# A fused mLSTM, attention and ConvFFN step on one core: a buffer, two loads and three norm steps are moved at the seams of the last two stages

## Chip, cores and metric

The kernel runs on one core of a Trainium2 chip. The metric is the device time of one execution in microseconds (us), as the median of repeated executions. A matmul runs on TensorE (PE; its weight loads are PEld), elementwise work on VectorE (DVE), ScalarE (ACT) and GpSimd (POOL), and SyncE (SP) issues most of the DMAs.

## What is computed

The reference is one layer of an encoder over 2048 prompt tokens and 8 x 16 sample tokens, 17 tiles of 128 tokens in all. Only its last part matters here:

```python
def conv_ffn(h, conv_prev, w_up, w_conv, b_conv, w_down):
    T = h.shape[1]
    u = h @ w_up
    ext = jnp.concatenate([conv_prev.astype(u.dtype), u], axis=1)
    c = b_conv + sum(ext[:, j:j + T] * w_conv[j] for j in range(CONV_W))
    a, g = jnp.split(c, 2, axis=-1)
    return (jax.nn.silu(g) * a) @ w_down, ext[:, -(CONV_W - 1):]
...
    y = layer_norm(DEEPNORM_ALPHA * h + f, ln2_g, ln2_b)
```

The width is 1024, `w_up` has 2 x 2816 columns (value and gate), and the convolution is causal with three taps. All is float32.

## The kernel before

**Products.** Every float32 operand is split into a rounded high part and the rest (`split`: a copy on ACT, L218, and a subtraction on DVE, L219), and a product is the sum high x high + high x low + low x high: three matmuls for one. On top of this the matrix products use a seven-product scheme in place of eight block products (the numbers 1 to 7 named `s` in the code).

**Blocks.** In the ConvFFN the tokens go in three blocks (`FBLOCKS`): tiles 0 to 5, 6 to 11 and 12 to 16. For each block the up-projection (`f_ups`) runs over 22 pairs `j` of a value row and a gate row, 128 columns of `w_up` each. The seven products of a pair (`f_product`, matmul at L1874) collect in three PSUM banks A, B and C of either `fup` (even `j`) or `dps` (odd `j`). `f_evict` takes them out: step 5 copies bank B into `ub` (ACT, L1902) and adds it to bank C to give the second half of the gate row `u1` (DVE, L1903 and L1905); step 4 then adds the rest of bank C, after its product has collected in the same bank, to give the first half (DVE, L1911). The value row goes to `u0`. `f_after` puts the two rows of state ahead of the row (POOL, L1925 and L1927), takes the three taps (ACT, L1929; DVE, L1931 twice), keeps the last rows (POOL, L1932 and L1934), and after the gate row calls `f_gate` (ACT, L1955; DVE, L1956 and L1957), whose result is stored from `cc` to DRAM (L1958, L1960). `u0` and `u1` have one buffer each, so pair `j + 1` can write its gate row only when pair `j` has read its own for the last time. The last pair of the last block has its products in the order 6, 5, 2, 3, 4, with product 4 of the pair before it between 6 and 5.

**Down-projection.** `f_downs` runs over `dseq`: for each block `b` the steps `s` in the order 1, 2, 4, 6, 5, 3, 7 (the last block: 1, 2, 4, 6, 5, 7, 3), and for each step six units `u` of two of the 11 row blocks (the last unit has one). The counter `g` runs over all 3 x 7 x 6 = 126 units. A unit needs split weights (`d_weights`, tile `uw`) and split tokens (`d_tokens`, tile `fu`; for some steps also sums of token quarters, L2038 to L2048). At unit `g` the code asks for the weights of unit `g + 4` and the tokens of unit `g + 5`; the split weights live in a ring of five pairs of buffers. The matmuls are at L2084. After the last unit of a step the result is added to the output rows `yacc` (`add`, L2113 and L2115). Tokens are loaded at L2002, weights at L2020, the rows of the residual at L2139.

**The last norm.** When a tile is complete, `finish` is put on the list `pending`. It is a generator in three pieces: the statistics (L1556 to L1558 on DVE, L1559 on POOL); subtract the mean and multiply by `ln2_g` (L2124); multiply by the scale and add `ln2_b` (L2126), and store (L2127). At each unit `g` the first two of the list go on by one piece. The last step of the last block (`s` = 3, three tiles) uses `norm_last` (L1542, L1544) instead. `ln2_g` and `ln2_b` are loaded at L2060, at the head of `f_downs`, into the two buffers of the tag `hst`, which have held token tiles for the transposes of `f_hT`.

**What sets the order.** PE runs in the order of the code. On every other engine and DMA queue the framework writes a fixed order at build time: it steps through a time of its own and takes, among the instructions that it holds ready, the one traced first; `high_priority` puts `f_evict`'s and `add`'s instructions ahead of others. Each engine then works through its queue in that order, and a waiting instruction holds what is behind it. Buffers of one tag go round in the order of the code.

## Time and profile before

| | |
|---|---|
| median of 3 runs | 2311.37 us |
| the three runs | 2311.37, 2309.41, 2311.43 us |
| the profiled execution, its own time | 2306.19 us |
| its span, first to last instruction | 2304.4 us |
| mean granted clock of PE | 0.997 |
| busy share of the span: DVE / ACT / POOL | 78% / 55% / 12% |

Times in the profile count from the first instruction of the span. A line of a timeline has the start, the time taken, the engine, the line of the program, the operation, the tile written and the tiles read, the shape, and how many were merged; in brackets stands how long the engine sat idle before it and what released it. A line of waits has the waiting engine, tile and line, the releaser, the sum of the idle time, how often, and the longest. A line of the chain of work that ended last has start, time and what.

### The profile page before, as it was taken

The numbers are of one execution on the slowest core, as the hardware profiler recorded it, in microseconds if no ns is written. First come the engines' busy times: TensorE is split into PE (matmuls) and PEld (weight loads), VectorE is DVE, ScalarE is ACT, GpSimd is POOL, SyncE is SP. The second block draws the span as 40 slices with busy tenths as digits, with TensorE's granted clock in tenths as the row PEclk, the third lists the DMA queues.
The fourth block names the chain that finished last, engine by engine and source line by source line (L and its number), as shares of the span: only waits on it lengthen the run. The fifth ranks groups of instructions, "written<-read, shape, count | busy, mean of one in ns | idle before, by whom it ended". The sixth has DMA issues, their size and how long they took to land.

```text
span 2304.4 us, 39746 instructions
## 1 busy us (share of the span) xinstructions
PE 2279.1 (99%) x14293; PEld 2093.5 (91%) x14293; DVE 1807.5 (78%) x3075; ACT 1272.6 (55%) x2377; POOL 272.7 (12%) x509
## 2 busy tenths in 40 slices
PE   8999999999999999999999999999999999999998
PEld 8999999999877778999999999999999988888876
DVE  8787587787688878998778777678766786895987
ACT  4453476776766656555656555555555544444442
POOL 0001001000011210211112100003111200100100
PEclk9999999999999999999999999999999999999999
DMA  7988999999987757888778889978998786756742
GB/s 265 320 303 298 311 321 342 312 305 345 313 285 241 239 196 278 306 320 307 277 276 279 302 307 308 320 263 290 318 293 262 230 294 214 256 167 222 254 154 84
DMA packets 300165, 632.38 MB, mean 274 GB/s; under 512 B 47868, under 2 KB 141120, under 8 KB 299968
## 3 DMA queue, kind: packets, MB, share of 16 engines
q1 hardware_dynamic: 295296, 616.14, 77.8%
q0 software_dynamic: 3520, 10.56, 1.4%
q10 hardware_dynamic: 1152, 3.15, 0.4%
q8 instruction: 113, 1.85, 0.3%
q14 instruction: 84, 0.69, 0.1%
HBM read 458.11 MB, written 171.64 MB: 273 GB/s over the span
## 4 chain that ended last, share of the span: by engine, by line
PE 81%; DVE 4%; DMA 1%; issue 1%; ACT 1%; POOL 0%; SPq 0%; DVEq 0%; ACTq 0%; POOLq 0%
PE dps L1874 19%; PE fup L1874 19%; PE dps L705 7%; PE fup L2084 7%; PE dps L2084 6%; PE fht L2084 6%; PE dps L223 3%; PE dps L224 2%; PE dps L225 2%; PE ppo L1349 1%; PE psc L1304 1%; PE ppt L1343 1%; PE dps L731 1%; PE fht L1698 1%; DVE w L219 1%
## 5 line engine op out<-in xcount | busy, mean ns | idle before, releaser
L1874 PE MATMUL dps<-hh,uw 128*128 128x384 f32 (+1 forms) x1848 | 478.0, 328 | 2.1 <-DVE u L1905 2.1
L1874 PE MATMUL fup<-hh,uw 128*128 128x384 f32 (+1 forms) x1848 | 478.0, 328 | 0.0
L1874 PEld LDWEIGHTS dps<-hh,uw 128*128 128x128 f32 x1848 | 330.0, 188 | 2.4 <-DVE u L1905 2.4
L1874 PEld LDWEIGHTS fup<-hh,uw 128*128 128x128 f32 x1848 | 330.0, 188 | 0.0
L1931 DVE SCALAR_TENSOR_TENSOR cc<-u,cw,cc 128x768 f32<-128x768 f32 (+1 forms) x264 | 257.9, 977 | 63.7 <-ACT cc L1929 56.9
L1874 PE MATMUL fup<-hl,uw 128*128 128x384 f32 (+1 forms) x924 | 302.7, 328 | 0.9 <-DVE hl L219 0.9
L1874 PE MATMUL dps<-hl,uw 128*128 128x384 f32 (+1 forms) x924 | 302.3, 327 | 0.0
L705 PE MATMUL dps<-w,oh 128*128 128x256 f32 x1344 | 254.2, 284 | 0.0
L218 ACT CAST uw<-wraw 128x1024 fp32r<-128x1024 f32 x126 | 123.2, 978 | 231.4 <-PE dps L2084 122.4
L219 DVE TENSOR_TENSOR w<-wraw,w 128x1024 fp32r<-128x1024 f32 (+2 forms) x167 | 189.3, 1140 | 67.0 <-ACT w L218 64.6
L218 ACT CAST w<-wraw 128x1024 fp32r<-128x1024 f32 (+2 forms) x167 | 163.0, 984 | 121.3 <-PE dps L705 63.4
L705 PEld LDWEIGHTS dps<-w,oh 128*128 128x128 f32 x1344 | 210.4, 188 | 10.9 <-issue 8.1
L219 DVE TENSOR_TENSOR uw<-wraw,uw 128x1024 fp32r<-128x1024 f32 x126 | 142.4, 1130 | 65.7 <-ACT uw L218 64.0
L705 PE MATMUL dps<-w,ol 128*128 128x256 f32 x672 | 187.8, 279 | 0.0
L1874 PEld LDWEIGHTS fup<-hl,uw 128*128 128x128 f32 x924 | 173.5, 188 | 1.6 <-DVE hl L219 1.5
L2084 PE MATMUL fup<-uw,fu 128*128 128x512 f32 x726 | 173.7, 396 | 0.0
L1874 PEld LDWEIGHTS dps<-hl,uw 128*128 128x128 f32 x924 | 173.5, 188 | 0.0
L705 PE MATMUL dps<-oh,w 128*128 128x256 f32 x896 | 169.7, 284 | 3.6 <-DVE w L219 1.3
L2084 PE MATMUL dps<-uw,fu 128*128 128x512 f32 x660 | 165.3, 396 | 1.1 <-DVE uw L219 1.1
L2084 PEld LDWEIGHTS fup<-uw,fu 128*128 128x128 f32 x726 | 136.3, 188 | 33.1
L1929 ACT ACTIVATE cc<-u,cw 128x768 f32<-128x768 f32 (+1 forms) x132 | 132.2, 1001 | 49.2 <-DVE u L1911 23.9
L2084 PEld LDWEIGHTS dps<-uw,fu 128*128 128x128 f32 x660 | 123.8, 188 | 31.5 <-DVE uw L219 1.5
(318 smaller groups left out, 4577.9 us busy)
## 6 DMA issues: line engine op xcount, KB each, us to landing
uw<-zw SPq DMA_DIRECT2D x176, 512.0 KB, 5.0
zw<-uw SPq DMA_DIRECT2D x88, 512.0 KB, 3.5
w<-zws SPq DMA_DIRECT2D x72, 512.0 KB, 5.9
wv<-wup SPq DMA_DIRECT2D x66, 512.0 KB, 4.6
wraw<-wi SPq DMA_DIRECT2D x65, 512.0 KB, 6.1
wraw<-zt SPq DMA_DIRECT2D x60, 512.0 KB, 3.9
wraw<-wdn SPq DMA_DIRECT2D x45, 512.0 KB, 4.5
wraw<-wo SPq DMA_DIRECT2D x40, 512.0 KB, 4.7
```

Of the source, the lines that this page charges most:

```text
L218: nc.scalar.copy(hi, src)
L219: nc.vector.tensor_sub(lo, src, hi.bitcast(F32))
L223: mm(out, ah, bh, start=start, stop=False)
L224: mm(out, ah, bl, start=False, stop=False)
L225: mm(out, al, bh, start=False, stop=stop)
L705: mm(o, l, r, start=s in (1, 7) and c == k == i == 0, stop=k == 3 and i == 2, skip_group_check=True)
L731: mm(o, x, w, start=k == i == 0, stop=k == KD - 1 and i == 2, skip_group_check=True)
L1304: nc.tensor.matmul(ps[kvh][:, j, :nk], q[rs, j0 + j], k[rs, sel], start=i == 0, stop=i == 2)
L1874: mm(ps, l[:, k], r[:, k], start=s in (1, 7) and k == 0 and i == 0, stop=k == 3 and i == 2, skip_group_check=True)
L1929: S.activation(c[:, v], u[:, 2:2 + n], AF.Identity, bias=w[3], scale=w[2])
L1931: V.scalar_tensor_tensor(c[:, v], u[:, i:i + n], w[i], c[:, v], op0=ALU.mult, op1=ALU.add)
L2084: mm(ps, l[:, k, c], r[:, k], start=s in (1, 4, 7) and u == 0 and k == 0 and i == 0, stop=u == nu - 1 and k == n - 1 and i == 2, skip_grou ...
```

## The change

Three edits. First, the gate row of the last pair of the last block is put into a buffer of the tag `hst` and not into `u1`. Second, the two loads of the norm's parameters are traced at `g` = 18, the first unit of the fourth step of the first block, and no longer at the head of `f_downs`. Third, in the last block the pieces of `finish` are traced at the end of the unit, after the weights and the tokens that the unit asks for, and within `issue_after(self.low)`: each DVE instruction that the piece traces is put behind the low-part subtraction of the latest weights in the queue. `split` returns that subtraction, and `d_weights` keeps it.

```diff
     def split(self, hi, lo, src):
         nc = self.nc
         nc.scalar.copy(hi, src)
-        nc.vector.tensor_sub(lo, src, hi.bitcast(F32))
+        return nc.vector.tensor_sub(lo, src, hi.bitcast(F32)).ins
...
         elif s == 5:
-            self.ug = u = half(1)
+            end = (b, j) == (len(FBLOCKS) - 1, NFF - 1)
+            self.ug = u = self.fp.tile([P, 770], F32, name="u1", tag="hst", bufs=2) if end else half(1)
...
-        self.split(hi[:, :n], lo[:, :n], raw[:, :n])
+        self.low = self.split(hi[:, :n], lo[:, :n], raw[:, :n])
...
         ln2 = []
-        for n in ("ln2_g", "ln2_b"):
-            t = self.fp.tile([P, D], F32, name="f_" + n, tag="hst", bufs=2)
-            nc.sync.dma_start(t, a[n].to_broadcast([P, D]))
-            ln2.append(t)
...
+        def step():
+            for f in pending[:2]:
+                if next(f, self) is self:
+                    pending.remove(f)
+
         for g, (b, s, u) in enumerate(self.dseq):
...
+            if g == 3 * nu:
+                for n in ("ln2_g", "ln2_b"):
+                    t = self.fp.tile([P, D], F32, name="f_" + n, tag="hst", bufs=2)
+                    nc.sync.dma_start(t, a[n].to_broadcast([P, D]))
+                    ln2.append(t)
...
-            for f in pending[:2]:
-                if next(f, self) is self:
-                    pending.remove(f)
+            if b < nb - 1:
+                step()
             if u == nu - 1 and not last:
                 for p in cols[::-1] if s == 7 else cols:
                     after(s, p)
...
                 self.d_tokens()
+            if b == nb - 1:
+                with self.tc.issue_after(self.low):
+                    step()
```

## The prediction

> **What bounds the kernel now.** I read the page first, then the waits of PE, then the chain of work around the two places that the change touches, and last the timelines of single engines there.

> ```profile
> span 2304.4 us, 39746 instructions
> PE 2279.1 (99%) x14293; PEld 2093.5 (91%) x14293; DVE 1807.5 (78%) x3075; ACT 1272.6 (55%) x2377; POOL 272.7 (12%) x509
> ...
> PE ppt L1518 <- POOL v L1094: 2.9, 1, 2.9
> PE dps L1874 <- DVE u L1905: 2.1, 1, 2.1
> ...
> PE dps L2084 <- DVE uw L219: 1.1, 1, 1.1
> ...
> PE fht L2084 <- DVE yacc L2115: 0.2, 1, 0.2
> ```

> PE is busy for 2279.1 of 2304.4 us, and the edits leave its matmuls alone. So the change can only win PE's idle time, 25.3 us over the whole span, and of that only what lies in the last two stages. There PE waits three times: 2.1 us for the gate row (L1905), 1.1 us for a weight split (L219), 0.2 us for an addition. The 2.9 us of L1518 belong to an earlier stage. After PE's last matmul come a last norm and its store. The third edit doesn't reach them, because `norm_last` is called inside the product loop as before. The most that the change can win is thus 2.1 + 1.1 + 0.2 = 3.4 us, 0.15% of the span.

> **Part 1, the gate row in its own buffer.** The first wait, from the chain, then from the timelines of ACT, PE and DVE:

> ```profile
> 1823.18 3.53 PE dps L1874 x24
> ...
> 1829.96 0.35 DVE u L1903
> 1830.31 0.21 DVE u L1905
> ...
> 1830.56 2.02 PE dps L1874 x12
> ```
> ```profile
> 1825.24 0.41 ACT L1902 COPY ub<-dps 128x320 f32<-128x320 f32 x1
> ```
> ```profile
> 1828.14 0.30 PE L1874 MATMUL dps<-hh,uw 128*128 128x320 f32 x1
> 1830.56 0.42 PE L1874 MATMUL dps<-hh,uw 128*128 128x320 f32 x1 [2.12 <-DVE u L1905]
> ```
> ```profile
> 1825.04 1.21 DVE L219 TENSOR_TENSOR uw<-wraw,uw 128x1024 fp32r<-128x1024 f32 x1
> 1826.18 0.89 DVE L1931 SCALAR_TENSOR_TENSOR cc<-u,cw,cc 128x656 f32<-128x656 f32 x1
> 1827.14 1.23 DVE L219 TENSOR_TENSOR uw<-wraw,uw 128x1024 fp32r<-128x1024 f32 x1
> 1828.28 0.90 DVE L1931 SCALAR_TENSOR_TENSOR cc<-u,cw,cc 128x656 f32<-128x656 f32 x1
> 1829.09 0.95 DVE L219 TENSOR_TENSOR fu<-r,fu 128x768 fp32r<-128x768 f32 x1
> 1829.96 0.35 DVE L1903 TENSOR_TENSOR u<-dps,ub 128x192 f32<-128x192 f32 x1
> ```

> The last pair's step 4 collects in the bank that L1903 and L1905 read, so PE waits for L1905. Their data is there at 1825.24 + 0.41 = 1825.65. They run 4.3 us later because `u1` still holds the row before, whose second tap (L1931) ends at 1828.28 + 0.90 = 1829.2. With a buffer of its own only `ub` is left to wait for. L1903 is high in priority, so it goes behind the split of 1825.04, which ends at 1826.25, and the two (0.35 + 0.21) are over by about 1826.9. PE wants the bank when its last matmul before the gap ends, 1828.14 + 0.30 = 1828.4: a cover of 1.5 us, and the 2.12 us go. Should one split more (1.23) get ahead of them, the cover still holds; should a tap get ahead as well (0.9), some 0.6 us of wait would stay. Bounds of this term: 0 to 2.12 us; I take 2.12. No instruction is added.

> What is late next? The first units of the down-projection have their splits done by then; the nearest is the first token unit of the second step:

> ```profile
> 1848.13 1.83 DVE L219 TENSOR_TENSOR fu<-r,fu 128x768 fp32r<-128x768 f32 x2
> ```
> ```profile
> 1833.06 46.20 PE fup L2084 x198
> ...
> 1883.46 2.80 PE dps L2084 x12
> ```
> ```profile
> 1831.00:2156.00 325.00, 325.00 (x1398) 261.63 (x1398) 260.06 (x314) 142.84 (x175) 18.72 (x19) 1.00 0.68 230
> ```
> ```profile
> 1876.47 1.22 DVE L219 TENSOR_TENSOR uw<-wraw,uw 128x1024 fp32r<-128x1024 f32 x1
> ```

> The 46.20 us are two steps of 99 matmuls, so the second begins at 1833.06 + 23.1 = 1856.2, and its tokens are split by 1850.0: 6.2 us of cover. The tightest that I find is the weight split of unit 13, over at 1877.7 for a product at 1883.46: 5.8 us, or 3.7 once PE comes 2.1 us earlier. Behind the seam PE is busy for 325.00 of 325 us (the row of a table by stretches: PE, PEld, DVE, ACT, POOL, clock, DMA share, GB/s), so the 2.12 us arrive at the end whole.

> **Part 2, the parameters loaded later.** Before, the loads went out long ahead:

> ```profile
> 1475.91 0.38 SPq L2060 DMA_DIRECT2D f_ln_g<-ln_g  x1
> ...
> 1492.10 0.38 SPq L2060 DMA_DIRECT2D f_ln_b<-ln_b  x1
> ```
> ```profile
> f_ln_g<-ln_g SPq DMA_DIRECT2D x1, 512.0 KB, 8.0
> ```
> ```profile
> L2124 DVE SCALAR_TENSOR_TENSOR yacc<-yacc,lmv,f_ln_g x14: 1271/1274/1279, 1977.1 to 2281.7; 128x1024 f32<-128x1024 f32 x14
> ```
> ```profile
> 1836.54 0.90 DVE L1931 SCALAR_TENSOR_TENSOR cc<-u,cw,cc 128x656 f32<-128x656 f32 x1
> ```
> ```profile
> 1843.88 4.24 SPq L2002 DMA_DIRECT2D r<-zf  x8
> ```
> ```profile
> 1860.00:1870.00 10.00, 10.00 (x45) 8.05 (x44) 8.99 (x11) 3.98 (x5) 0.00 (x0) 1.00 1.05 405
> ```

> One `hst` buffer now holds the gate row until its last tap ends at 1836.54 + 0.90 = 1837.4, so at least one load falls behind that. First use is L2124 at 1977.1, far off. On SP each issue takes 0.38 us, and the row loads behind it wait until 1843.88 anyway. A load is 0.5 MB; at 405 GB/s the two take 2.6 us of DMA time, in a stretch where the DMA engines are full. That is under the 3.7 us of cover left at unit 13: cost 0. From the other side, if everything behind were late by each load's 8.0 us to land, 16 us, it would break the cover (a rival below). Taking the loads away from 1476 to 1492 wins nothing, since PE has no wait there. I take 0, as the bandwidth row is that of the stretch itself. [...]

> **Part 3, the norm steps behind the splits.** Around the second wait, DVE, ACT and PE:

> ```profile
> 2274.27 1.22 DVE L219 TENSOR_TENSOR uw<-wraw,uw 128x1024 fp32r<-128x1024 f32 x1
> 2275.41 0.95 DVE L219 TENSOR_TENSOR fu<-r,fu 128x768 fp32r<-128x768 f32 x1
> 2276.28 1.87 DVE L1556 BATCH_NORM_STATS2 lst<-yacc 128x6 f32<-128x512 f32 x3
> ...
> 2278.78 1.22 DVE L219 TENSOR_TENSOR uw<-wraw,uw 128x1024 fp32r<-128x1024 f32 x1
> ...
> 2280.52 2.47 DVE L2124 SCALAR_TENSOR_TENSOR yacc<-yacc,lmv,f_ln_g 128x1024 f32<-128x1024 f32 x2
> 2282.91 0.68 DVE L219 TENSOR_TENSOR uw<-wraw,uw 128x512 fp32r<-128x512 f32 x1
> ```
> ```profile
> 2276.77 0.62 ACT L218 CAST uw<-wraw 128x512 fp32r<-128x512 f32 x1 [2.45 <-PE fht L2084]
> ```
> ```profile
> 2283.64 0.73 PE L2084 MATMUL dps<-uw,fu 128*128 128x512 f32 x2 [1.08 <-DVE uw L219]
> ```

> The three `uw` rows are the weights of units 123, 124 and 125. The last has its high part at 2277.4 and could be split then, but stands behind both L2124; PE pays 1.08 us. Does the edit turn this round? I follow the code. Before, the tiles come on the list at the end of unit 119; the pieces run in units 120, 121, 122, each ahead of the weights that its unit asks for (124, 125, none). After, they run at the end of units 119, 120, 121, behind weights 123, 124, 125. Both give: weights 123, statistics, weights 124, L2124, weights 125, L2126. The edges ask only for what the order has already: L2124 behind weights 124, not 125. So the wait stays, and this part gives 0 here; its bounds are 0 and 1.08.

> It does move something at the start of the last block, where three tiles of the block before are still on the list: their pieces go from ahead of the weights of units 88 to 93 to behind them. DVE's work is the same in sum. A split needs its buffers freed by PE, so the pieces wait a few us more; but behind them stand splits wanted four units (16.8 us) later, and no matmul waits for the norm: 0.

> **Sum.** 2306.19 - 2.12 = 2304.1 us for an execution like the profiled one (span 2302.3). The median shown, 2311.37, is 5.2 us above that execution, so the same step on it gives 2309.25, said as 2309.3 us: 0.09% less.

> **The rivals.**
> - *Both waits go*: the framework's order, made from its own times, puts weights 125 ahead of L2124. For it: the high part is there 3.1 us before L2124 starts. Against: the code traces L2124 first. 2311.37 - 2.12 - 1.08 = 2308.2 us.
> - *The change doesn't do what it says*: something else holds L1903, such as a second tap and splits queued ahead of it, so that PE waits as long. For it: between 1825 and 1830 DVE has hardly a gap. Against: the priority of `f_evict`. 2311.4 us.
> - *Slower: the late loads starve the weights.* If each load holds back what is behind it by its 8.0 us, unit 13 is late by 16 - 3.7 = 12.3 us; less 2.1 gained, the time is 2311.4 + 10.2 = 2321.6 us. It decides from the point where the delay passes 3.7 us, and the kernel is slower than before past 5.8 us. For it: the DMA engines are full there. Against: 2.6 us of traffic.

> **Chances and range.** Forecast 0.70, both waits 0.12, no gain 0.12, slower 0.06. The three runs lie 2.0 us apart, and the profiled execution lies 5.2 below their median, so a median can be off by 2 to 3 us. Low: 2308.2 less half of 5.2, 2305.6. High: no gain plus half of 2.0, 2312.4; the slow rival is left out. A measurement of this kernel tells about 0.2% (4.6 us) from no change. Faster by more needs a median under 2306.7, beyond even both waits: 0.11, by the scatter. Slower by more: 0.06. Within: 0.83.

> **What would show it.** Part 1: PE's wait for L1905 gone, L1903 near 1826, the down-projection starting near 1831. Part 2: one load at least behind 1835, no wait of PE at L2084 between 1831 and 2200. Part 3: the wait for L219 still about 1.1 us, with L2124 ahead of the 512-wide split. I am wrong if a new wait shows behind 1831, or if the splits at the end stand in another order.

## The result and the profile after

| | before | after |
|---|---|---|
| median | 2308.07 us (22 runs, 2303.73 to 2311.43) | 2305.24 us (22 runs, 2302.08 to 2310.27) |
| profiled execution, its own time | 2306.19 us | 2306.25 us |
| its span | 2304.4 us | 2304.5 us |

The ratio is 0.9987, with a 95% interval of 0.9981 to 0.9992: the change takes off 2.8 us (1.8 to 4.4). The interval leaves out a change of nothing, and the difference is inside the 0.2% (4.6 us) that the prediction gave as most likely. The predicted 2309.3 us lies 4.1 us above the median measured, and the low end of the range 0.4 us above it.

The lines of the program have moved a little: L1903, L1905 and L1931 are now L1904, L1906 and L1932; the matmul L2084 is L2081, the copies L2092 are L2089, L2124 is L2121, and the loads of the norm's parameters stand at L2145.

The two profiled executions have the same span, so the change is to be read stage by stage. First the waits of PE in the kernel after, around the seam and to its end:

```profile
PE fup L2081 <- ACT fht L2089: 1.2, 1, 1.2
...
PE dps L2081 <- DVE uw L219: 1.1, 1, 1.1
```

The 2.1 us at L1905 are gone, and the 1.1 us for the weight split are still there. New is a wait of 1.2 us at the second step of the down-projection, where PE needs a bank that ACT's copies (L2089) have not yet emptied.

**The seam.** DVE in the kernel after, and then two moments of PE in each kernel (the product 4 of the pair before the last, and the first matmul of the down-projection), before first:

```profile
1826.01 1.22 DVE L219 TENSOR_TENSOR uw<-wraw,uw 128x1024 fp32r<-128x1024 f32 x1
1827.14 0.35 DVE L1904 TENSOR_TENSOR u<-dps,ub 128x192 f32<-128x192 f32 x1
1827.41 0.28 DVE L1906 TENSOR_TENSOR u<-dps,ub 128x128 f32<-128x128 f32 x1
1827.61 0.89 DVE L1932 SCALAR_TENSOR_TENSOR cc<-u,cw,cc 128x656 f32<-128x656 f32 x1
```
```profile
1821.25 0.31 PE L1874 MATMUL fup<-hh,uw 128*128 128x320 f32 x1
...
1832.89 1.33 PE L2084 MATMUL fup<-uw,fu 128*128 128x512 f32 x5
```
```profile
1822.21 0.32 PE L1874 MATMUL fup<-hh,uw 128*128 128x320 f32 x1
...
1831.48 1.79 PE L2081 MATMUL fup<-uw,fu 128*128 128x512 f32 x7
```

The gate row's additions now stand ahead of the second tap, one split later than forecast, and PE does not wait for them. From product 4 to the first matmul of the down-projection it was 1832.89 - 1821.25 = 11.64 us and is 1831.48 - 1822.21 = 9.27 us: 2.37 us less. I call this stretch the seam. The wait read 2.12 us in the trace; the seam lost more, because the last matmul ahead of the gap is recorded as 0.30 us long and the first behind it as 0.42 us, while such matmuls otherwise start 0.17 us apart or less (12 of them in 2.02 us, by the chain before).

**Behind it.** From the first matmul of the down-projection to the end of the span it was 2304.4 - 1832.89 = 471.5 us and is 2304.5 - 1831.48 = 473.0 us: 1.5 us more. That is where the gain went. ACT in the kernel after, then PE:

```profile
1849.15 0.84 ACT L218 CAST fu<-r 128x768 fp32r<-128x768 f32 x1 [3.84 <-DMA r<-zf]
...
1852.09 0.84 ACT L218 CAST fu<-r 128x768 fp32r<-128x768 f32 x1 [0.42 <-DMA r<-zf]
1853.61 0.83 ACT L218 CAST fu<-r 128x768 fp32r<-128x768 f32 x1 [0.69 <-DMA r<-zf]
1854.35 1.04 ACT L218 CAST uw<-wraw 128x1024 fp32r<-128x1024 f32 x1
1855.30 1.06 ACT L2089 COPY fht<-fup 128x512 f32<-128x512 f32 x2
```
```profile
1855.93 6.34 PE L2081 MATMUL fup<-uw,fu 128*128 128x512 f32 x26 [1.21 <-ACT fht L2089]
```

The copies start 1855.30 - 1831.48 = 23.8 us behind the first matmul of the step, whose 99 matmuls take 23.1 us. Ahead of them in ACT's queue stand token casts that wait for row loads (`r<-zf`). In the kernel before, with the first matmul at 1832.89, the copies came at 22.2 us:

```profile
1854.09 1.05 ACT L218 CAST uw<-wraw 128x1024 fp32r<-128x1024 f32 x1 [1.44 <-PE fup L2084]
1855.05 1.06 ACT L2092 COPY fht<-fup 128x512 f32<-128x512 f32 x2
```

There the cast ahead of them waited for PE itself, not for a load. The first of the two copies was over at about 1855.6, half of 1.06 us behind 1855.05, and PE wanted its bank at 1832.89 + 23.1 = 1856.0: a cover of 0.4 us, which the prediction had not looked for.

Why do the rows come later? SP's queue in the kernel after, and the time that the last store of the convolution's rows took to land, after and before:

```profile
1837.68 0.33 SPq L2145 DMA_DIRECT2D f_ln_b<-ln_b  x1
1838.72 0.38 SPq L2021 DMA_DIRECT2D wraw<-zt  x1
1840.34 0.33 SPq L1959 DMA_DIRECT2D zf<-cc  x1
1840.72 0.43 SPq L1961 DMA_DIRECT2D zf<-cc  x1
1842.17 0.37 SPq L2021 DMA_DIRECT2D wraw<-zt  x1
1845.79 3.94 SPq L2003 DMA_DIRECT2D r<-zf  x8
```
```profile
zf<-cc SPq DMA_DIRECT2D x1, 64.0 KB, 5.0
```
```profile
zf<-cc SPq DMA_DIRECT2D x1, 64.0 KB, 3.1
```

What the row loads waited for in SP's queue, from 1835 to 1850 us, after and before:

```profile
SPq L2003 <- DMA zf<-cc: 3.1, 2, 2.4
```
```profile
SPq L2002 <- DMA zf<-cc: 2.5, 2, 1.8
```

The row loads read what the store of 1840.72 writes, so they start when it has landed. It lands in 5.0 us where it took 3.1, and 3.0 us ahead of it the 512 KB of `ln2_b` (tile `f_ln_b`) are issued. By the packets in the trace these run from 1838.87 to 1842.63 us, and those of the store begin 2.5 us behind its issue, where they began 1.5 us behind it before. The trace has the packets of both on one queue (q1). Whether the store shares the DMA engines with the load or stands behind it in that queue, no run here tells; that it is this load is shown below (one_behind). Together with the seam (the store now starts 9.2 us behind the first matmul, before 1840.72 - 1832.89 = 7.8) the row loads begin 14.3 us behind the first matmul, before 11.0.

**The end.** DVE in the kernel after, and PE:

```profile
2280.55 2.47 DVE L2121 SCALAR_TENSOR_TENSOR yacc<-yacc,lmv,f_ln_g 128x1024 f32<-128x1024 f32 x2
2282.94 0.68 DVE L219 TENSOR_TENSOR uw<-wraw,uw 128x512 fp32r<-128x512 f32 x1
```
```profile
2283.67 0.73 PE L2081 MATMUL dps<-uw,fu 128*128 128x512 f32 x2 [1.08 <-DVE uw L219]
```

The same order and the same 1.08 us as before: the third part does nothing here.

### The profile page after: what moved, and what is told of

Same layout as the page of the kernel before. It is cut to its first block, busy times and chain, and to the rows that moved or that the text cites. A ratio compares the mean times of both kernels' runs of the same rounds, so it can differ in the third digit from the quotient of the medians.

```text
span 2304.5 us, 39741 instructions
## 1 busy us (share of the span) xinstructions
PE 2278.9 (99%) x14293; PEld 2094.4 (91%) x14293; DVE 1807.4 (78%) x3075; ACT 1272.4 (55%) x2377; POOL 279.4 (12%) x509
## 4 chain that ended last, share of the span: by engine, by line
PE 81%; DVE 4%; DMA 2%; issue 1%; ACT 1%; POOL 0%; SPq 0%; DVEq 0%; ACTq 0%; POOLq 0%
PE dps L1874 19%; PE fup L1874 19%; PE dps L705 8%; PE fup L2081 6%; PE dps L2081 6%; PE fht L2081 6%; PE dps L223 3%; PE dps L224 2%; PE dps L225 2%; PE ppo L1349 1%; PE psc L1304 1%; PE ppt L1343 1%; PE dps L731 1%; PE fht L1698 1%; PE pscore L1129 1%
## 5 line engine op out<-in xcount | busy, mean ns | idle before, releaser
L1874 PE MATMUL fup<-hh,uw 128*128 128x384 f32 (+1 forms) x1848 | 478.4, 328 | 0.0
L1874 PE MATMUL dps<-hh,uw 128*128 128x384 f32 (+1 forms) x1848 | 478.0, 328 | 0.0
L1874 PEld LDWEIGHTS fup<-hh,uw 128*128 128x128 f32 x1848 | 330.5, 188 | 0.0
L1874 PEld LDWEIGHTS dps<-hh,uw 128*128 128x128 f32 x1848 | 330.3, 188 | 0.0
L1932 DVE SCALAR_TENSOR_TENSOR cc<-u,cw,cc 128x768 f32<-128x768 f32 (+1 forms) x264 | 258.2, 979 | 62.8 <-ACT cc L1930 56.1
L1874 PE MATMUL fup<-hl,uw 128*128 128x384 f32 (+1 forms) x924 | 303.2, 328 | 0.9 <-DVE hl L219 0.9
L1874 PE MATMUL dps<-hl,uw 128*128 128x384 f32 (+1 forms) x924 | 302.8, 328 | 0.0
L705 PE MATMUL dps<-w,oh 128*128 128x256 f32 x1344 | 254.2, 284 | 0.0
L218 ACT CAST uw<-wraw 128x1024 fp32r<-128x1024 f32 x126 | 123.3, 979 | 230.4 <-PE dps L2081 122.4
L219 DVE TENSOR_TENSOR w<-wraw,w 128x1024 fp32r<-128x1024 f32 (+2 forms) x167 | 189.7, 1142 | 66.0 <-ACT w L218 61.9
L218 ACT CAST w<-wraw 128x1024 fp32r<-128x1024 f32 (+2 forms) x167 | 163.0, 984 | 119.0 <-PE dps L705 61.9
L705 PEld LDWEIGHTS dps<-w,oh 128*128 128x128 f32 x1344 | 210.7, 188 | 10.8 <-issue 8.1
L219 DVE TENSOR_TENSOR uw<-wraw,uw 128x1024 fp32r<-128x1024 f32 x126 | 142.5, 1131 | 62.3 <-ACT uw L218 62.2
L705 PE MATMUL dps<-w,ol 128*128 128x256 f32 x672 | 188.1, 280 | 0.0
L1874 PEld LDWEIGHTS fup<-hl,uw 128*128 128x128 f32 x924 | 173.9, 188 | 1.7 <-DVE hl L219 1.5
L2081 PE MATMUL fup<-uw,fu 128*128 128x512 f32 x726 | 174.0, 396 | 1.2 <-ACT fht L2089 1.2
L1874 PEld LDWEIGHTS dps<-hl,uw 128*128 128x128 f32 x924 | 173.8, 188 | 0.0
L705 PE MATMUL dps<-oh,w 128*128 128x256 f32 x896 | 169.6, 285 | 3.6 <-DVE w L219 1.3
L2081 PEld LDWEIGHTS fup<-uw,fu 128*128 128x128 f32 x726 | 136.6, 188 | 34.3 <-ACT fht L2089 1.6
L2081 PE MATMUL dps<-uw,fu 128*128 128x512 f32 x660 | 165.3, 396 | 1.1 <-DVE uw L219 1.1
L1930 ACT ACTIVATE cc<-u,cw 128x768 f32<-128x768 f32 (+1 forms) x132 | 132.0, 1001 | 46.2 <-DVE u L1912 22.2
L2081 PEld LDWEIGHTS dps<-uw,fu 128*128 128x128 f32 x660 | 124.1, 188 | 31.2 <-DVE uw L219 1.5
## 6 DMA issues: line engine op xcount, KB each, us to landing
uw<-zw SPq DMA_DIRECT2D x176, 512.0 KB, 5.1
zw<-uw SPq DMA_DIRECT2D x88, 512.0 KB, 3.3
w<-zws SPq DMA_DIRECT2D x72, 512.0 KB, 5.8
wv<-wup SPq DMA_DIRECT2D x66, 512.0 KB, 4.4
wraw<-wi SPq DMA_DIRECT2D x65, 512.0 KB, 5.5
wraw<-zt SPq DMA_DIRECT2D x60, 512.0 KB, 4.1
wraw<-wdn SPq DMA_DIRECT2D x45, 512.0 KB, 4.5
wraw<-wo SPq DMA_DIRECT2D x40, 512.0 KB, 4.7
```

Source lines behind the costliest of these rows:

```text
L218: nc.scalar.copy(hi, src)
L219: return nc.vector.tensor_sub(lo, src, hi.bitcast(F32)).ins
L705: mm(o, l, r, start=s in (1, 7) and c == k == i == 0, stop=k == 3 and i == 2, skip_group_check=True)
L1874: mm(ps, l[:, k], r[:, k], start=s in (1, 7) and k == 0 and i == 0, stop=k == 3 and i == 2, skip_group_check=True)
L1930: S.activation(c[:, v], u[:, 2:2 + n], AF.Identity, bias=w[3], scale=w[2])
L1932: V.scalar_tensor_tensor(c[:, v], u[:, i:i + n], w[i], c[:, v], op0=ALU.mult, op1=ALU.add)
```

## The experiments

All of these kernels compute the full result. "Seam" and "to the end" are the two stretches above, from the profile of each kernel. The difference in time is the ratio less 1, times the median of before that was run beside the kernel.

| kernel | median (runs), before beside it | ratio (95%) | difference, us | seam | to the end |
|---|---|---|---|---|---|
| row_dead | 2305.77 (11), 2308.44 | 0.9989 (0.9980 to 0.9998) | -2.5 | 9.26 | 471.5 |
| loads_behind | 2306.29 (11), 2308.44 | 0.9995 (0.9987 to 1.0004) | -1.2 | 9.26 | 471.5 |
| no_row | 2309.34 (11), 2308.44 | 1.0003 (0.9994 to 1.0012) | +0.7 | 12.35 | 472.3 |
| norm_behind | 2307.27 (11), 2308.44 | 0.9999 (0.9990 to 1.0007) | -0.2 | 13.12 | 470.7 |
| after_again | 2307.70 (11), 2308.89 | 0.9993 (0.9985 to 1.0002) | -1.6 | 9.26 | 473.1 |
| fill_gap | 2308.36 (11), 2308.89 | 0.9999 (0.9991 to 1.0008) | -0.2 | 11.65 | 471.5 |
| wide_gap | 2314.91 (10), 2308.89 | 1.0021 (1.0011 to 1.0030) | +4.8 | 18.85 | 471.8 |
| dead_behind | 2305.91 (11), 2308.89 | 0.9985 (0.9975 to 0.9995) | -3.5 | 9.26 | 470.7 |
| one_behind | 2306.02 (10), 2309.51 | 0.9983 (0.9974 to 0.9993) | -3.9 | 9.26 | 471.5 |
| row_hst | 2306.32 (10), 2309.51 | 0.9988 (0.9978 to 0.9997) | -2.8 | 9.26 | 475.9 |
| steps_only | 2308.08 (10), 2309.51 | 0.9999 (0.9989 to 1.0009) | -0.2 | 11.65 | 471.5 |
| before_again | 2308.36 (10), 2309.51 | 0.9996 (0.9986 to 1.0005) | -0.9 | 11.64 | 471.5 |
| row_hst_again | 2307.33 (10), 2308.18 | 0.9997 (0.9987 to 1.0006) | -0.7 | 9.26 | 472.4 |
| after_third | 2306.05 (10), 2308.18 | 0.9992 (0.9983 to 1.0002) | -1.8 | 9.26 | 472.3 |
| before_third | 2308.14 (10), 2308.18 | 1.0002 (0.9993 to 1.0012) | +0.5 | 12.35 | 472.4 |

The runs beside these experiments are not those of the table of the result. The intervals are about 4 us wide, so times alone separate few of these kernels; the two copies of the kernel before show -0.9 and +0.5 us. The stretches of the profile decide, and the times are held against their sum.

### The gate row without the late loads

The kernel before, with the gate row in the buffer `hh5`, which holds no live tile by then, so that the norm's parameters load early as before:

```diff
-            self.ug = u = half(1)
+            end = (b, j) == (len(FBLOCKS) - 1, NFF - 1)
+            self.ug = u = f2.tile([P, 770], F32, name="u1", tag="hh5", bufs=1) if end else half(1)
```

> The kernel before with one edit: the last pair's gate row goes into the buffer of the tokens of product 5, which are dead by then. The parameters keep their early loads and the norm steps their place. The gate row's wait (2.4 us start to start) goes by both theories. Theory A (the parameters' late loads delay the token rows, and ACT's copies behind them make PE wait 1.2 us at the second step): no wait of PE for the copies of L2089; 2.4 us faster, ratio about 0.9990. Theory B (the delay comes from the weights load that now stands ahead of the token rows on SP, which this kernel has too): the wait for the copies stays at 0.5 to 1.2 us; 1.0 to 1.9 us faster, ratio about 0.9994.

Measured: seam 9.26 us, to the end 471.5 us as in before, no wait for the copies, 2.5 us faster. With this buffer the first part wins its whole gap; the loss behind the seam does not come from an earlier start of the down-projection alone.

### The loads behind the row loads

The kernel after, with both norm loads queued behind the row loads of the first step:

```diff
-        self.nc.sync.dma_start(r[:, ks, :h], z[:, :, c0:c0 + h])
+        self.rows = self.nc.sync.dma_start(r[:, ks, :h], z[:, :, c0:c0 + h]).ins
...
-                    nc.sync.dma_start(t, a[n].to_broadcast([P, D]))
+                    with self.tc.issue_after(self.rows):
+                        nc.sync.dma_start(t, a[n].to_broadcast([P, D]))
```

> The changed kernel with its two parameter loads put behind the token row loads of the first block on SP's queue; the weights load ahead of the rows stays. Theory A: the first row load goes out near 1844 instead of 1845.8, no wait of PE for the copies, 1.2 to 1.4 us faster than the changed kernel's profile, ratio to before about 0.9990. Theory B: rows still late by over 1 us and a wait of 0.5 to 1.2 us at the copies.

The waits of PE from the seam to the end of this kernel, and the landing of the last store:

```profile
PE dps L2081 <- DVE uw L219: 1.1, 1, 1.1
PE fht L2081 <- DVE yacc L2112: 0.2, 1, 0.2
```
```profile
zf<-cc SPq DMA_DIRECT2D x1, 64.0 KB, 3.3
```

No wait for the copies, the store lands in 3.3 us, and the row loads start 12.6 us behind the first matmul, in the changed kernel 14.3. The weight load that stands ahead of the row loads is still there, so it is not what costs. The time, 1.2 us less than before, is not as good as the forecast; that is left open below.

### Only the second load behind

The same edit for `ln2_b` alone:

```diff
-                    nc.sync.dma_start(t, a[n].to_broadcast([P, D]))
+                    with self.tc.issue_after(self.rows) if n == "ln2_b" else nullcontext():
+                        nc.sync.dma_start(t, a[n].to_broadcast([P, D]))
```

> The changed kernel with one load alone, ln2_b, queued behind the row loads of the down-projection's first step; ln2_g stays among the weight loads ahead of it. Theory (the copies of the first step's result, L2089 on ACT, wait because the token casts ahead of them wait for row loads that the ln2_b load has pushed back): the first row load is issued at most 13.3 us behind the first down-projection matmul (14.3 in the changed kernel, 13 or less where both loads lie behind), and PE's wait for the copy in the first 30 us of the down-projection, 1.2 us in the changed kernel twice, is under 0.4 us. Rival (the load of ln2_g, or any load among the weights, costs as much): the row load is still about 14.3 us behind, and the wait 0.6 to 1.2 us. Time by the theory 1.2 us under the changed kernel's, ratio to before about 0.999; by the rival as the changed kernel.

Measured: the row loads start 12.5 us behind the first matmul, there is no wait for the copies, to the end 471.5 us, 3.9 us faster. `ln2_g`, which goes out at the start of the seam, is harmless; the new wait is the work of `ln2_b`, issued just ahead of the last stores. This is the changed kernel without its new wait; by their times alone the two cannot be told apart.

### Without the first part, and the third part alone

no_row is the kernel after with the gate row back in `u1`:

```diff
-            end = (b, j) == (len(FBLOCKS) - 1, NFF - 1)
-            self.ug = u = self.fp.tile([P, 770], F32, name="u1", tag="hst", bufs=2) if end else half(1)
+            self.ug = u = half(1)
```

> The changed kernel without its first edit: the gate row is back in u1, the loads are traced late, the norm steps stand behind the splits. If the first edit is all that acts, PE waits 2.1 us for the gate row as before, the parameters load near 1476 and 1492 as before, and the time is that of the kernel before, ratio 0.9995 to 1.0005. Rival: the second and third edits win something of their own (the measured gain of 2.8 us is more than the 2.1 forecast): 0.5 to 1 us faster, ratio about 0.9997.

steps_only is the kernel before with the pieces of the norm traced as after:

```diff
-            for f in pending[:2]:
-                if next(f, self) is self:
-                    pending.remove(f)
+            if b < nb - 1:
+                step()
...
+            if b == nb - 1:
+                with self.tc.issue_after(self.low):
+                    step()
```

> Part 3 alone: the norm's steps of the last block queued behind the splits, the gate row in u1 and the loads early. All theories: the wait for the gate row 2.1 us and the wait for the weight split before the last steps 1.1 us stay, no wait for the copies; ratio to before 0.9995 to 1.0010. Open: whether the gap also halves the clock of PE behind it (two of three kernels with the gap so far): if so the seam takes 12.3 to 13.2 us or the first matmuls of the down-projection are slow, and if not it takes 11.64.

Measured: both have the gap of 2.12 us and the 1.1 us at the end, and neither is faster than before. With the gate row in `u1` the two `hst` buffers are free, and the loads go out early wherever they are traced. So the second part costs nothing by its place in the code; it is the first part's buffer that makes the second load late. no_row showed a surprise: its seam took 12.35 us, not 11.64, with the clock at 0.50 behind the gap. That is taken up below.

### The first edit alone, in the buffer of the changed kernel

The gate row in the `hst` buffer, and all else as before: the loads are traced at the head of `f_downs`, and still go out late, because one of their two buffers holds the gate row:

```diff
-            self.ug = u = half(1)
+            end = (b, j) == (len(FBLOCKS) - 1, NFF - 1)
+            self.ug = u = self.fp.tile([P, 770], F32, name="u1", tag="hst", bufs=2) if end else half(1)
```

> Parts 1 and 2 without part 3: the gate row in the hst buffer, the two loads traced at the head of the down-projection, the norm's steps as before. Theory (the buffer that the row takes pushes the loads back, whatever the place where they are traced): the seam takes 9.26 us as in the changed kernel, and the wait for the copies (1.2 us) is there in full. Rival (the place where the loads are traced, or part 3, brings the wait of the copies): that wait is under 0.4 us. Ratio to before 0.9987 to 0.9995 by the theory.

> Parts 1 and 2 again (the gate row in the hst buffer, no part 3). Open: its first profile had a wait of 2.55 us for the copies, behind which the clock fell to 0.50 for 3.41 us, while its median was 0.12% under the kernel before. Theory (the wait comes from row loads that land late, so its length differs from execution to execution, from about 1.2 us up): here it lies between 0.5 and 2.6 us, with DMA as releaser of the token casts ahead of the copies. Rival (without part 3 the wait is always 2.5 us): 2.5 us again. Clock, by the theory of windows: PE's clock is looked at in a fixed grid of 3.413 us windows, the grid being that of the profile's other low stretches; the window behind one with under about 1.45 us of busy PE runs at 0.50, behind one with over 1.63 us at 1.00.

The wait of PE for the copies, in row_hst and then in its second profile:

```profile
PE fup L2085 <- ACT fht L2093: 2.5, 1, 2.5
```
```profile
PE fup L2085 <- ACT fht L2093: 0.6, 1, 0.6
```

The wait is there without the second and the third edit, and its length differs from execution to execution of one program. The rival, a fixed 2.5 us without part three, falls.

### The changed kernel again

> The changed kernel once more, for a second profile. By the measure from the start of the pair before the last's product 4 to the first matmul of the down-projection, called the seam: 9.3 us and clock 1.00 there, as in its first profile. If the wait at the copies (1.35 us start to start) belongs to the kernel and not to one execution, it is there again, 1.0 to 1.5 us, and from the first matmul of the down-projection to the end it takes 473 us; if it was an accident, 471.5 us. Time against before: ratio 0.998 to 0.9995.

> The changed kernel, unchanged, a third profile. Theory: the wait for the copies is there again, 0.5 to 2.6 us; below 1.7 us of it the clock stays at 1.00. Rival (it is a fixed 1.2 us): 1.2 us again. Ratio to before 0.998 to 0.9995.

Measured: a wait for the copies of 1.2 us in the second profile and of 0.5 us in the third, whose row is:

```profile
PE fup L2081 <- ACT fht L2089: 0.5, 1, 0.5
```

It belongs to the kernel and is not fixed. In all five profiles that have the second load ahead of the stores (three of the changed kernel, two of row_hst) the store took 4.7 to 5.4 us to land (5.0, 5.4 and 4.9, then 5.3 and 4.7); in five without it 3.1 to 3.3 (before 3.1, before_third 3.2, row_dead 3.2, dead_behind 3.1, loads_behind 3.3). In before_again, no_row and fill_gap, which lack it too, the row loads that wait for the store begin 3.1 to 3.3 us behind its issue.

### The norm's steps really behind the last weights

The third part meant to spare PE the last split. This kernel is before with the pieces of the last step queued behind the last weight split:

```diff
-            for f in pending[:2]:
-                if next(f, self) is self:
-                    pending.remove(f)
+            if not last:
+                step()
...
+            if last:
+                with self.tc.issue_after(self.low):
+                    step()
```

> The kernel before with the norm pieces of the last step only traced at the end of their unit and queued behind the latest weight split, so that L2124 stands behind the weights of the last unit. If the 1.1 us wait before the last products is the price of that order, it goes, PE ends 1.1 to 1.2 us earlier and the kernel is 1.1 to 1.2 us faster, ratio about 0.9995. Rival: VectorE is the bound in the last 25 us, its work is only reordered and the end stays: ratio 1.000, with PE idle elsewhere or the last norm late by as much.

The last additions on DVE in this kernel:

```profile
2297.03 0.74 DVE L1544 SCALAR_TENSOR_TENSOR yacc<-yacc,lsc,f_ln_b 128x512 f32<-128x512 f32 x1
2298.37 0.69 DVE L2113 SCALAR_TENSOR_TENSOR yacc<-yacc,fht 128x512 f32<-128x512 f32 x1 [0.60 <-PE fht L2084]
2298.98 0.74 DVE L1544 SCALAR_TENSOR_TENSOR yacc<-yacc,lsc,f_ln_b 128x512 f32<-128x512 f32 x1
```

The wait of 1.1 us is gone and the way to the end is 470.7 us, 0.8 less. The rest is given back: a last piece of the tile before (2298.98) now stands between the last addition and the last tile's statistics, and from the last addition to the end it takes 7.9 us, before 7.4. The time itself (-0.2 us, -2.3 to +1.6) does not tell this kernel from before.

### Both waits removed

row_dead and norm_behind together.

> The two edits that worked alone together: the gate row in the dead token buffer, the norm pieces of the last step behind the last weight split. Seam 9.3 us, no wait at the copies, no wait before the last products; from the first matmul of the down-projection to the end 470.7 us (471.5 less the 0.8 that the order of the norm won). Against before 2.4 to 3.9 us at the seam and 0.8 at the end: 3.2 to 4.7 us faster, ratio about 0.9983; if seam and end don't add, 0.9990.

Measured: seam 9.26, to the end 470.7, both as short as in any kernel here; 3.5 us faster (1.2 to 5.8). Its time cannot be told from one_behind's.

### The gap filled, and the gap widened

fill_gap puts 15 matmuls into the gap, whose result nothing reads; wide_gap writes the second half of the gate row seven times. Both start from the kernel before.

```diff
+            if (b, j, s) == (nb - 1, NFF - 1, 4):
+                hole = self.fup.tile([P, 512], F32, name="fht", tag="fht", bufs=2)
+                for _ in range(15):
+                    nc.tensor.matmul(hole[:, :320], self.wc[b, j, s][0][:, 0], self.hc[b, s][0][:, 0], start=True, stop=True, skip_group_check=True)
```
```diff
-            V.tensor_add(u[:, 2 + h:2 + WP], C[:, :m], u4[:, :m])
+            for _ in range(7 if (b, j) == (len(FBLOCKS) - 1, NFF - 1) else 1):
+                V.tensor_add(u[:, 2 + h:2 + WP], C[:, :m], u4[:, :m])
```

> The kernel before with 15 more matmuls of PE (results unused, in a free PSUM bank) in the place where it waits for the gate row, 2.2 us in all, so that PE is busy in the gap. Theory G (in part of the executions the gap also halves PE's granted clock for some 3 us, which costs 0.8 to 1.5 us more): the seam takes 11.6 to 11.9 us and the clock is 1.00 from 1830 to 1840. Theory S (the longer seams are scatter of VectorE's work and not of the clock's gate): the seam is as in the kernel before, 11.6 to 13.1 us, and a lower clock may show. The time is that of before or up to 1 us less.

> The kernel before with the second half of the last pair's gate row written seven times instead of once (the same values), which makes VectorE 1.6 us later there, so that PE's gap at the seam is about 4 us instead of 2.4. Theory G: the clock is 0.5 behind the gap for about 3.4 us, and the seam takes 11.6 + 1.6 + 1.5 = 14.5 to 15 us. Theory S: clock 1.00, the seam takes 13.2 us, or up to 14.7 with the same scatter. 1.6 to 3 us slower than before, ratio 1.0007 to 1.0013.

Measured: filled, the seam keeps its 11.65 us and the clock stays at 1.00. Widened, PE waits 7.4 us, not 4, because DVE's queue puts splits, taps and the gate's steps between the seven additions. The clock is at 0.50 for 10.2 us, and the kernel is 4.8 us slower (2.5 to 6.9). The seam is 7.2 us longer than in a profile of before at full clock; the runs of before that stand beside it may include some whose clock falls as well, as it does in before_third below.

### The kernel before again

> The kernel before, unchanged, for another profile of it. Ratio 1.000 within 0.001. If the gap of 2.1 to 2.4 us halves PE's clock in some executions of a kernel and not by the kernel's code, this profile may show either 11.64 us for the seam at a clock of 1.00 throughout, as the first profile of it did, or 12.3 to 13.2 us with slices of 0.50 to 0.72 within 6 us behind the gap. If it is the code, it must be 11.64 again.

> The kernel before, unchanged, a third profile. All theories: the wait for the gate row is 2.12 us. Theory of windows: the clock falls to 0.50 for 3.41 us if and only if one window of the fixed grid holds about 1.9 us or more of the gap, and the seam with the first product then takes 1.4 to 1.7 us more; else the seam is 11.64 us. Rival (chance, with no bearing on the grid): the two don't go together.

before_again has a seam of 11.64 us at full clock, before_third one of 12.35 us with the clock at 0.50 behind the gap: the same program shows both. With no_row, norm_behind and steps_only there are six profiles with this gap, three of either kind.

What tells them apart? In before the trace has a clock of 0.50 in three stretches: from 10.58 us for 6.83 us, from 41.30 us for 3.41 us, and from 2300.93 us to the end. Their starts lie 30.72 and 2259.62 us apart, which is 9 and 662 steps of 3.4133 us; the changed kernel has the same two distances, from 10.18 to 40.90 and on to 2300.52 us. So I lay a grid of windows of this length over each profile, with one edge at the start of one of its low stretches. Here it is over the gap by a table of stretches (PE, PEld, DVE, ACT, POOL, clock, DMA share, GB/s), in before, steps_only, no_row and before_third:

```profile
1826.47:1829.89 3.42, 1.98 (x14) 1.72 (x12) 3.35 (x4) 1.97 (x6) 1.61 (x3) 1.00 0.61 166
1829.89:1833.30 3.41, 2.74 (x16) 2.60 (x17) 3.32 (x8) 1.58 (x4) 1.81 (x5) 1.00 0.62 231
```
```profile
1828.34:1831.76 3.42, 1.64 (x12) 1.38 (x10) 3.35 (x5) 2.17 (x5) 1.62 (x5) 1.00 0.60 192
1831.76:1835.17 3.41, 3.07 (x18) 2.84 (x19) 3.32 (x7) 1.59 (x3) 1.47 (x3) 1.00 0.62 235
```
```profile
1830.34:1833.76 3.42, 1.44 (x10) 1.44 (x11) 3.42 (x7) 2.81 (x5) 2.77 (x6) 1.00 0.57 195
1833.76:1837.17 3.41, 3.41 (x11) 2.83 (x11) 2.96 (x5) 0.93 (x1) 0.00 (x0) 0.50 0.41 153
1837.17:1840.58 3.41, 3.41 (x16) 2.77 (x15) 2.39 (x3) 0.00 (x0) 0.00 (x0) 1.00 0.48 118
```
```profile
1830.57:1833.98 3.41, 1.45 (x10) 1.45 (x11) 3.41 (x7) 2.79 (x5) 2.76 (x6) 1.00 0.60 199
1833.98:1837.40 3.42, 3.42 (x11) 2.84 (x11) 2.98 (x5) 0.93 (x1) 0.00 (x0) 0.50 0.42 155
```

In before and steps_only the gap is shared out between two windows, PE is busy for 1.98 and 1.64 us of the emptier one, and the clock stays at 1.00. In no_row and before_third one window holds nearly all of the gap, PE is busy for 1.44 and 1.45 us of it, and the window behind runs at 0.50: 11 matmuls in it, where the next one of no_row at 1.00 has 16. norm_behind goes with these two (1.41 us busy, then 0.50), and so does row_hst, whose wait of 2.5 us lay within one window (0.88 us busy, then 0.50). In the changed kernel the wait of 1.2 us left PE busy for 2.21 us of its window, and the clock stayed at 1.00. The last two, row_hst first:

```profile
1852.39:1855.81 3.42, 0.88 (x4) 0.38 (x2) 2.40 (x3) 3.14 (x5) 0.00 (x0) 1.00 1.05 398
1855.81:1859.22 3.41, 3.40 (x8) 2.75 (x9) 2.41 (x3) 3.07 (x5) 0.00 (x0) 0.50 1.05 407
```
```profile
1853.37:1856.78 3.41, 2.21 (x10) 1.47 (x9) 2.73 (x3) 3.17 (x5) 0.00 (x0) 1.00 1.04 393
1856.78:1860.20 3.42, 3.42 (x16) 2.77 (x15) 2.55 (x3) 2.21 (x5) 0.00 (x0) 1.00 1.05 405
```

before_third was profiled after these two bounds had been put down as an expectation, and agrees with them. In fill_gap the 15 matmuls run from 1834.65 to 1837.00 us, wholly within one window of its grid:

```profile
1833.86:1837.27 3.41, 3.41 (x24) 3.22 (x23) 3.41 (x7) 2.42 (x5) 1.89 (x5) 1.00 0.82 279
1837.27:1840.69 3.42, 3.42 (x21) 3.05 (x20) 3.42 (x6) 1.02 (x2) 0.88 (x2) 1.00 0.47 170
```

Without them nearly the whole gap would have lain in that window, as in no_row; with them the clock behind it stays at 1.00. One profile, but it speaks for the reading that the fall goes with PE's idle time in the window. The two bounds, 1.45 and 1.64 us, are however those of this place. Near the start of before, where PE runs other matmuls (L705), 1.90 us of busy PE were not enough:

```profile
37.89:41.30 3.41, 1.90 (x14) 1.49 (x13) 3.41 (x6) 2.95 (x4) 0.00 (x0) 1.00 0.98 393
41.30:44.71 3.41, 3.41 (x18) 3.41 (x18) 3.41 (x6) 0.94 (x1) 0.00 (x0) 0.50 0.70 223
```

Busy time as the profile models it thus does not tell all cases apart, and what else counts was not shown. What the window at 0.50 cost is read from no_row and before_third: 0.7 us more in the seam and 0.8 us more to the end, 1.5 us. In norm_behind it falls into the seam as a whole (13.12 against 11.64).

## Why the prediction was right or wrong

**Part 1** was right in its mechanism and too small in its size. The wait went, the additions moved ahead of the tap, the cover held with one split more ahead of them, and the down-projection began at 1831.48 where 1831 was forecast. The term of 2.12 us measured 2.37 us start to start (2.4 in every pair of profiles at full clock), and 3.9 us where the clock fell to 0.50 behind the gap (2.37 + 1.5). With three of six profiles of either kind, an estimate is 3.1 us a run. By a second estimate, from the windows above, a gap of 2.12 us laid at random on a grid of 3.41 us leaves 1.9 us or more of itself in one window (between 3.41 - 1.64 and 3.41 - 1.45) in about half of the cases, which fits three of six. The prediction took the idle time of one profiled execution for the price of the gap; that execution was one that kept its clock at 1.00 there.

**Part 2** failed at the step "cost 0". The check behind it looked for what is late next among splits (6.2 us of cover for tokens, 3.7 for weights), and reckoned the loads as 2.6 us of traffic against that. The tightest consumer was another: the copies on ACT, with 0.4 us of cover, which do not need the rows but stand in the queue behind casts that do. Two things used the cover up. The seam got shorter, and the stores and row loads did not move up with it (1.4 us), which alone is not enough, as row_dead shows. And the load of `ln2_b` delayed a 64 KB store, which landed in 4.7 to 5.4 us and not in 3.1 to 3.3, and the row loads wait for that store. The cost is what the way to the end grew by: 1.5, 1.5 and 0.8 us in three profiles. Two readings led there. The prediction took it as given that the row loads "wait until 1843.88 anyway", but what they wait for is the store that the load delays. And the row of 405 GB/s is of 1860 to 1870, not of the stretch where the load ran: in before, the DMA share of the three us from 1837 lies between 0.20 and 0.53. It was not the second edit that made the load late but the buffer that the first one takes (row_hst). The rival "slower: the late loads starve the weights" had the right cause, late loads that hold back what is behind them, but the wrong victim and ten times the price. The prediction priced only the bytes of the loads (2.6 us). What counted was one small transfer behind that of `ln2_b`, one that had a reader in wait. The forecast "no wait of PE at L2084 between 1831 and 2200" is refuted, as it had named for the case that it was wrong.

**Part 3** was right: the same order at the end, the same 1.08 us, and no gain in steps_only. The displaced steps at the start of the last block cost PE nothing that the trace shows. norm_behind adds that the rival "both waits go" was overpriced, at 1.08 us: with the split ahead, 0.8 us is left, because a piece of the tile before now stands ahead of the last tile's steps.

**The sum.** By the profiles the change should win 3.1 us and lose 1.3 us (the mean of 1.5, 1.5 and 0.8): 1.8 us. The three measurements of the changed kernel gave -2.8 (-4.4 to -1.8), -1.6 (-3.5 to +0.5) and -1.8 us (-3.9 to +0.5). The forecast of -2.1 us lies within all three, but by two errors of opposite sign: a gain too small by 1.0 us and a loss left out.

**The step onto the median** is the one that failed for the time, and it put the forecast beyond its range. The prediction subtracted from 2311.37 us, the median of three runs, having seen that the profiled execution lay 5.2 us below it. Over 22 runs the kernel before has a median of 2308.07 us, and the three shown contain its highest. From there the same step gives 2306.0 us. Of the 4.0 us by which 2309.25 was too high, 3.3 are this level and 0.7 the change, which took off 2.8 us and not 2.1. The low end of the range allowed half of 5.2 us, 2.6, for the level, and 1.1 us more for both waits going.

**What stays open.** row_hst was 2.8 us faster in one measurement and 0.7 us in another, while its two profiles lost 4.4 and 0.9 us behind the seam; how long its wait is on the average was not settled. loads_behind has the same stretches as row_dead and one_behind (9.26 and 471.5 us), and measured only 1.2 us (3.0 to -0.9) of gain, where they let one expect 3.1. Executions also differ by some us ahead of the seam: the seam starts at 1821.25, 1821.97 and 1823.22 us in the three profiles of before. The mean granted clock goes with the whole time: of the 121 runs of before beside the experiments, the 9 at a mean clock of 0.999 have a median of 2306.4 us, the 33 at 0.998 of 2306.9, the 37 at 0.997 of 2308.9, the 35 at 0.996 of 2310.1 and the 6 at 0.995 of 2311.2. The profile of loads_behind, its slowest run (2311.28 us), has a clock of 0.99 from 1500 to 1815 us, where those of before and after have 1.00. Whether other gaps ahead of the seam make the level scatter in the way of this one was not shown; no run here changed one of them.

## What to carry to other kernels

When a step is brought forward or a load moved, look for what is late next among everything in the queues of that stretch, not only among the operands of the next matmuls: an instruction that needs nothing of the delayed data can stand behind one that does, as ACT's copies did here behind casts for which ACT sat idle 3.84, 0.42 and 0.69 us. Here a 512 KB load issued 3.0 us ahead of a 64 KB store whose reader was waiting cost the store's delay (4.7 to 5.4 us to land, not 3.1 to 3.3), not the load's own bytes. The gap on PE, too, cost more than its idle time (2.37 or 3.9 us for 2.12), so compare start to start over a whole stretch, in more than one profile, and hang an absolute time on more than three runs.
